# The four column tiles of each modulation product in reversed order, three of them pinned behind the one before

## The chip, the core and the metric

The kernel runs on one core of a Trainium2 chip. The metric is the device time of one execution in microseconds; the time before is the median of 3 runs, 1778.3 us (1777.71 to 1779.84). All data are float32.

## The reference, cut to what matters

One step of a two-layer diffusion backbone on 512 latent tokens and 128 context tokens, width 1024. Each layer derives six modulation vectors (shift, scale and gate, for attention and for the feed-forward part) from two conditioning vectors, `c` for latent and `c_ctx` for context tokens:

```
def modulation(cond, w_mod, b_mod):
    m = jax.nn.silu(cond) @ w_mod + b_mod        # (N, 1024) @ (1024, 6144)
    return jnp.split(m[:, None, :], 6, axis=-1)
...
h = rms_norm(x, norm_attn) * (1.0 + sc_a) + sh_a
proj = h @ w_in                                  # then two kinds of attention
x = x + g_a * (attention(proj) @ w_out)
h = rms_norm(x, norm_ffn) * (1.0 + sc_f) + sh_f
gate, up = jnp.split(h @ w_gate_up, 2, axis=-1)
x = x + g_f * ((jax.nn.silu(gate) * up) @ w_down)
```

The change touches only how `silu(cond) @ w_mod` is computed; the large products, `h @ w_in` and the like, run on the same engine around it.

## The kernel before

Activations are kept transposed, channels on the 128 partitions. Every large product is done three times with operands split into a high and a low part (`prod`, L476 to L478): ScalarE copies the high part of a weight (L83, tile `whi`), VectorE subtracts to get the low part (L84, `wlo`), and TensorE accumulates high by high, high by low and low by high. A weight tile comes by DMA from SyncE's queue (L449, `raw`, two buffers).

Order: `run` goes through start, projections, attention, output projection and feed-forward part of layer 0, then of layer 1. The modulation is laid beside the large products as generators: `step(side)` lets one advance by one `yield` after a block of products. Which instruction stands where in an engine's queue is then settled by the framework's scheduler, which plays the program through on a simulated timeline and prefers what was written earlier among what is ready. `tc.keep_in_program_order(ins)` adds one edge: `ins` may not be placed ahead of the instruction of its engine that was written last before it. It adds no semaphore and doesn't forbid others to come between.

Two parts compute modulation with column tiles, that is, products with only 32 output columns which use one quarter of TensorE's columns each. Tile j writes partitions 32j to 32j+31 of one accumulator (`mm`, two buffers).

- `mod` (L249), once, in the projections of layer 0, for 2048 of the 6144 columns. For each of 8 chunks k of 128 channels, four loads L263 of 256 KB bring 512 columns each into a `Q` buffer (six buffers in all), and four products L266 (weights `cT`, moving operand the loaded tile) accumulate into one bank. After k=7 VectorE copies the bank (L272), TensorE transposes it.
- `mod_sums` (L284), beside the output projection and the feed-forward part of layer 0, for the other eight groups of 1024 columns. VectorE multiplies each loaded chunk with the conditioning vector as a scalar per partition and adds up (L312 for k=0, L310 for the others, 128x512, four tiles `Q`, two for each conditioning vector), in eight steps of k. These sums are pinned with `keep_in_program_order`. Then `mod_store` (L321) sums over the partitions with four products L327 (weights `ones`, moving operand one of the four sums), copies the bank (L330, VectorE), transposes it (L333) and adds the bias (L339).

L619 and L643 are the end of the key heads on VectorE and the transposes of the keys on TensorE, L990 and L923 VectorE's readers of the large products in the feed-forward part.

Of the kernel before, what the change touches and what calls it, by code (L numbers as in the profile page):

```python
# [19 lines left out]
P = 128  # L20
D = 1024
KC = D // P
# [21 lines left out]
class Net:  # L44
# [153 lines left out]
    def start(self):  # L198
# [14 lines left out]
        acc = [self.S() for _ in range(3)]  # L213
        mod = self.start_mod(0)
        next(mod)
        for k in range(KC):
            next(mod)
            self.norm_scale(state, k)
            self.norm_chunk(state, k, 0, NT, rb)
            if k < KC - 1:  # L220
                mod = self.start_mod(k + 1)
                next(mod)
            if k % 2 == 0:
                wh = self.t([P, 2, 512], "whi", F32R, bufs=4)
                wl = self.t([P, 2, 512], "wlo", F32R, bufs=4)
                for b in range(2):
                    c = slice(256 * b, 256 * b + 256)
                    self.split(wh[:, :, c], wl[:, :, c], self.raw0[b][:, k:k + 2])
            for t in range(NTILE):
                o = acc[t // 2][:, 512 * (t % 2):512 * (t % 2) + 512]  # L230
                c, w = slice(t * P, (t + 1) * P), k % 2
                for i, (l_, r_) in enumerate(((hi, wh), (hi, wl), (lo, wh))):
                    nc.tensor.matmul(o, lhsT=l_[k][:, c], rhs=r_[:, w], start=k == 0 and i == 0,  # L233
                                     stop=k == KC - 1 and i == 2)
# [14 lines left out]
    def mod(self, l, g, place):  # L249

        nc = self.nc
        acc = self.mm()
        for k in range(KC):
            src = self.ins["w_mod"][l, k * P:(k + 1) * P, g * 2048:(g + 1) * 2048]
            if place == "Q":
                dst = [self.t([P, 512], "Q", bufs=6) for _ in range(4)]
            else:
                if k == 0:
                    self.ring = self.t([P, 2, 2048], "V")
                dst = [self.ring[:, k % 2]]  # L260
            n = 2048 // len(dst)
            for i, d in enumerate(dst):
                nc.sync.dma_start(d, src[:, i * n:(i + 1) * n])  # L263
            for j in range(4):
                c = j * 512
                nc.tensor.matmul(acc[32 * j:32 * j + 32, :], lhsT=self.cT[:, k, :],  # L266
                                 rhs=dst[c // n][:, c % n:c % n + 512],
                                 start=(k == 0), stop=(k == KC - 1), tile_position=(0, 32 * j))
            if k < KC - 1:
                yield  # L270
        m = self.t([P, 512], "P", bufs=3)
        nc.vector.tensor_copy(m, acc)  # L272
        pt = self.mm()
        for i in range(4):
            nc.tensor.transpose(pt[:, i * P:(i + 1) * P], m[:, i * P:(i + 1) * P], self.ident)
        for c in range(2):

            src = pt.rearrange("p (i j c) -> p j i c", i=4, j=4)[:, :, :, c]
            dst = self.modT[l][:, 16 * g:16 * g + 16, c].rearrange("p (j i) -> p j i", i=4)
            bias = self.vec[l][:, 16 * g:16 * g + 16].rearrange("p (j i) -> p j i", i=4)  # L280
            nc.vector.tensor_tensor(dst, src, bias, ALU.add)
        yield
# [38 lines left out]
    def mod_store(self, l, which, acc):  # L321
        nc = self.nc
        s = self.mm()
        for c in range(2):
            for i in range(2):
                j = 32 * (2 * c + i)
                nc.tensor.matmul(s[j:j + 32], lhsT=self.ones.broadcast_to([P, 32]), rhs=acc[c][i], start=True,  # L327
                                 stop=True, tile_position=(0, j))
        m = self.t([P, 512], "P", bufs=3)
        nc.vector.tensor_copy(m, s)  # L330
        pt = self.mm()
        for i in range(4):
            nc.tensor.transpose(pt[:, i * P:(i + 1) * P], m[:, i * P:(i + 1) * P], self.ident)  # L333
        for c in range(2):

            src = pt.rearrange("p (i c h r) -> p c h i r", i=4, c=2, h=2)[:, c, :, :, 0]
            dst = self.modT[l][:, KC * which:KC * which + KC, c].rearrange("p (h i) -> p h i", i=4)
            bias = self.vec[l][:, KC * which:KC * which + KC].rearrange("p (h i) -> p h i", i=4)
            nc.vector.tensor_tensor(dst, src, bias, ALU.add)  # L339
# [750 lines left out]
```

## Time and profile before

| | |
|---|---|
| median of 3 runs | 1778.3 us (1777.71 to 1779.84) |
| the profiled execution | 1776.35 us, its span 1774.6 us |
| TensorE busy | 1724.7 us (97%) |
| VectorE busy | 1014.1 us (57%) |
| ScalarE, GpSimd busy | 615.6 us, 277.6 us |
| granted TensorE clock, mean | 0.989 |

Times inside the profile are microseconds from the start of the span. A matmul's record lasts from its issue to the modelled end of its result, so records of one engine overlap, and the pitch from start to start tells what an instruction costs in a stream. In the timeline neighbours of one line are merged: "x2" with one duration is a run of two records.

### The profile page before, as it was taken

The numbers are of one execution on the slowest core, as the hardware profiler recorded it, in microseconds if no ns is written. First come the engines' busy times: TensorE is split into PE (matmuls) and PEld (weight loads), VectorE is DVE, ScalarE is ACT, GpSimd is POOL, SyncE is SP. The second block draws the span as 40 slices with busy tenths as digits, with TensorE's granted clock in tenths as the row PEclk, the third lists the DMA queues.
The fourth block names the chain that finished last, engine by engine and source line by source line (L and its number), as shares of the span: only waits on it lengthen the run. The fifth ranks groups of instructions, "written<-read, shape, count | busy, mean of one in ns | idle before, by whom it ended". The sixth has DMA issues, their size and how long they took to land.

```text
span 1774.6 us, 29153 instructions
## 1 busy us (share of the span) xinstructions
PE 1724.7 (97%) x12194; PEld 1609.7 (91%) x12194; DVE 1014.1 (57%) x1757; ACT 615.6 (35%) x1143; POOL 277.6 (16%) x266
## 2 busy tenths in 40 slices
PE   8889999999999999999999998999999999999999
PEld 6767978888999999899999997888999999999998
DVE  5765667877577877723247885778463232223222
ACT  4422376732422121212235434767252212221220
POOL 0332634400000000000002354453010000000000
PEclk9999999999999999999999999999999999999999
DMA  9343211153155554412222211112212222121212
GB/s 350 109 154 98 55 25 25 49 182 127 56 187 168 162 201 154 145 70 72 77 82 86 81 34 45 31 40 75 72 48 95 72 72 78 66 96 51 93 54 78
DMA packets 44259, 169.20 MB, mean 95 GB/s; under 512 B 5600, under 2 KB 8416, under 8 KB 32864
## 3 DMA queue, kind: packets, MB, share of 16 engines
q1 hardware_dynamic: 44128, 167.34, 28.5%
q8 instruction: 96, 1.57, 0.4%
q14 instruction: 35, 0.29, 0.1%
HBM read 152.90 MB, written 3.93 MB: 88 GB/s over the span
## 4 chain that ended last, share of the span: by engine, by line
PE 91%; DVE 3%; ACT 3%; DMA 1%; issue 1%; POOL 1%; SPq 0%; DVEq 0%; POOLq 0%; ACTq 0%
PE S L476 23%; PE S L477 23%; PE S L478 23%; PE S L687 3%; PE mm L792 3%; PE S L771 2%; PE S L688 2%; PE mm L327 2%; PE mm L788 2%; PE S L233 2%; PE mm L266 1%; PE mm L476 1%; PE mm L477 1%; PE mm L478 1%; DVE mx L707 1%
## 5 line engine op out<-in xcount | busy, mean ns | idle before, releaser
L83 ACT ACTIVATE whi<-raw 128x1024 fp32r<-128x1024 f32 (+2 forms) x192 | 196.2, 1025 | 811.2 <-PE S L477 734.8
L477 PE MATMUL S<-q,whi 128*128 128x256 f32 (+1 forms) x1408 | 436.3, 310 | 0.0
L478 PE MATMUL S<-k,wlo 128*128 128x256 f32 (+1 forms) x1408 | 434.6, 309 | 0.0
L476 PE MATMUL S<-k,whi 128*128 128x256 f32 (+1 forms) x1408 | 432.5, 310 | 1.5 <-ACT k L86 1.4
L84 DVE TENSOR_TENSOR wlo<-raw,whi 128x1024 fp32r<-128x1024 f32 (+2 forms) x192 | 229.9, 1200 | 183.1 <-ACT whi L83 175.9
L476 PEld LDWEIGHTS S<-k,whi 128*128 128x128 f32 x1408 | 265.5, 189 | 12.4 <-issue 10.1
L477 PEld LDWEIGHTS S<-q,whi 128*128 128x128 f32 x1408 | 266.7, 189 | 4.2 <-issue 4.2
L478 PEld LDWEIGHTS S<-k,wlo 128*128 128x128 f32 x1408 | 266.0, 189 | 2.5 <-issue 2.5
L478 PE MATMUL S<-hi,wlo 128*128 128x384 f32 (+1 forms) x768 | 237.9, 310 | 0.0
L477 PE MATMUL S<-lo,whi 128*128 128x384 f32 (+1 forms) x768 | 237.7, 310 | 0.0
L476 PE MATMUL S<-hi,whi 128*128 128x256 f32 (+1 forms) x768 | 237.7, 311 | 0.0
L923 DVE SCALAR_TENSOR_TENSOR x<-S,modT,x 128x128 f32<-128x128 f32 (+2 forms) x137 | 66.4, 524 | 208.6 <-PE S L478 208.6
L310 DVE SCALAR_TENSOR_TENSOR Q<-V,cT,Q 128x512 f32<-128x512 f32 x224 | 152.3, 743 | 0.0
L476 PE MATMUL S<-whi,hi 128*128 128x256 f32 x512 | 147.6, 288 | 1.9 <-ACT Q L241 1.9
L476 PEld LDWEIGHTS S<-hi,whi 128*128 128x128 f32 x768 | 144.0, 188 | 5.9 <-issue 5.0
L478 PEld LDWEIGHTS S<-hi,wlo 128*128 128x128 f32 x768 | 144.5, 188 | 3.4 <-issue 3.4
L478 PE MATMUL S<-whi,lo 128*128 128x256 f32 x512 | 145.8, 286 | 0.0
L477 PE MATMUL S<-wlo,hi 128*128 128x256 f32 x512 | 145.8, 285 | 0.0
L707 DVE TENSOR_REDUCE mx<-S 128x1 f32<-128x768 f32 x128 | 119.1, 950 | 46.3 <-PE S L688 46.0
L477 PEld LDWEIGHTS S<-lo,whi 128*128 128x128 f32 x768 | 144.4, 188 | 0.8 <-issue 0.8
L990 DVE TENSOR_TENSOR P<-S,P 128x640 f32<-128x640 f32 x44 | 36.2, 823 | 148.1 <-PE S L478 148.1
L476 PEld LDWEIGHTS S<-whi,hi 128*128 128x128 f32 x512 | 97.8, 191 | 8.2 <-issue 3.4
(206 smaller groups left out, 2820.7 us busy)
## 6 DMA issues: line engine op xcount, KB each, us to landing
raw<-in_w_gate_up SPq DMA_DIRECT2D x44, 1024.0 KB, 4.8
V<-in_w_mod SPq DMA_DIRECT2D x64, 512.0 KB, 3.9
raw<-in_w_in SPq DMA_DIRECT2D x16, 1024.0 KB, 4.8
raw<-in_w_down SPq DMA_DIRECT2D x16, 1024.0 KB, 5.0
Q<-in_w_mod SPq DMA_DIRECT2D x32, 256.0 KB, 3.1
raw<-in_w_out SPq DMA_DIRECT2D x8, 1024.0 KB, 5.1
raw<-in_w_down SPq DMA_DIRECT2D x8, 768.0 KB, 4.3
raw<-raw SPq DMA_DIRECT2D x40, 128.0 KB, 2.2
```

The source lines that it names most:

```text
L83: nc.scalar.activation(hi, src, AF.Copy)
L84: nc.vector.tensor_tensor(lo, src, hi.bitcast(F32), ALU.subtract)
L233: nc.tensor.matmul(o, lhsT=l_[k][:, c], rhs=r_[:, w], start=k == 0 and i == 0, stop=k == KC - 1 and i == 2)
L310: ins = nc.vector.scalar_tensor_tensor(a, v, self.cT[:, k, c:c + 1], a, ALU.mult, ALU.add)
L476: self.nc.tensor.matmul(out, lhsT=lh, rhs=rh, start=(i == 0), stop=False)
L477: self.nc.tensor.matmul(out, lhsT=lh, rhs=rl, start=False, stop=False)
L478: self.nc.tensor.matmul(out, lhsT=ll, rhs=rh, start=False, stop=(i == n - 1))
L687: nc.tensor.matmul(out, lhsT=Q[j][:, cols], rhs=keys[:, k0:k0 + n], start=True, stop=False)
L707: nc.vector.tensor_reduce(mx, s[:, 0:n], AX.X, ALU.max, negate=True)
L792: nc.tensor.matmul(o[64 * j:64 * j + 64], lhsT=self.V[:, v, 512 + 64 * j:576 + 64 * j], rhs=pts[j][:, i * P:(i + 1) * P], start=first, sto ...
L923: self.nc.vector.scalar_tensor_tensor(x[:, s:e], src[:, s - a:e - a], self.m(l, which, mb, c), x[:, s:e], ALU.mult, ALU.add)
L990: nc.vector.tensor_tensor(sg, out[1], sg, ALU.mult)
```

## The change

In `mod` and in `mod_store` the four column tiles are written in the order 3, 2, 1, 0 in place of 0 to 3, and tiles 2, 1 and 0 are each pinned behind the product written before, which is the next higher tile. Tile 3 is not pinned. Operands, shapes, loads and sums stay the same.

```diff
             for i, d in enumerate(dst):
                 nc.sync.dma_start(d, src[:, i * n:(i + 1) * n])
-            for j in range(4):
+            for j in reversed(range(4)):
                 c = j * 512
-                nc.tensor.matmul(acc[32 * j:32 * j + 32, :], lhsT=self.cT[:, k, :],
-                                 rhs=dst[c // n][:, c % n:c % n + 512],
-                                 start=(k == 0), stop=(k == KC - 1), tile_position=(0, 32 * j))
+                ins = nc.tensor.matmul(acc[32 * j:32 * j + 32, :], lhsT=self.cT[:, k, :],
+                                       rhs=dst[c // n][:, c % n:c % n + 512],
+                                       start=(k == 0), stop=(k == KC - 1), tile_position=(0, 32 * j))
+
+                if j < 3:
+                    self.tc.keep_in_program_order(ins)
...
     def mod_store(self, l, which, acc):
         nc = self.nc
         s = self.mm()
-        for c in range(2):
-            for i in range(2):
-                j = 32 * (2 * c + i)
-                nc.tensor.matmul(s[j:j + 32], lhsT=self.ones.broadcast_to([P, 32]), rhs=acc[c][i], start=True,
-                                 stop=True, tile_position=(0, j))
+
+        for j in reversed(range(4)):
+            ins = nc.tensor.matmul(s[32 * j:32 * j + 32], lhsT=self.ones.broadcast_to([P, 32]), rhs=acc[j // 2][j % 2],
+                                   start=True, stop=True, tile_position=(0, 32 * j))
+            if j < 3:
+                self.tc.keep_in_program_order(ins)
```

## Rows read from the trace of the kernel before

**Rows 1.** The page: TensorE's busy time and share; shares of the chain that ended last.

```profile
PE 1724.7 (97%) x12194; PEld 1609.7 (91%) x12194; DVE 1014.1 (57%) x1757; ACT 615.6 (35%) x1143; POOL 277.6 (16%) x266
...
PE 91%; DVE 3%; ACT 3%; DMA 1%; issue 1%; POOL 1%; SPq 0%; DVEq 0%; POOLq 0%; ACTq 0%
```

**Rows 2.** L266 and L327 by themselves: duration in ns (least/median/most), first and last start.

```profile
L266 PE MATMUL mm<-Q,cT x64: 592/605/617, 80.9 to 160.5; 128*32 128x512 f32 x64
...
L327 PE MATMUL mm<-Q,ones x64: 592/604/617, 418.6 to 758.0; 128*32 128x512 f32 x64
```

**Rows 3.** TensorE's timeline, a lone tile of L266: start, duration, line, tiles.

```profile
118.51 0.28 PE L477 MATMUL S<-wlo,hi 128*128 128x256 f32 x1
118.63 0.28 PE L478 MATMUL S<-whi,lo 128*128 128x256 f32 x1
118.84 1.04 PE L266 MATMUL mm<-Q,cT 128*32 128x512 f32 x2
...
120.04 0.28 PE L477 MATMUL S<-wlo,hi 128*128 128x256 f32 x1
```

**Rows 4.** TensorE's timeline, a lone tile of L327.

```profile
517.92 0.34 PE L477 MATMUL S<-q,whi 128*128 128x384 f32 x1
518.10 0.34 PE L478 MATMUL S<-k,wlo 128*128 128x384 f32 x1
518.37 1.05 PE L327 MATMUL mm<-Q,ones 128*32 128x512 f32 x2
...
519.63 0.34 PE L477 MATMUL S<-q,whi 128*128 128x384 f32 x1
```

**Rows 5.** TensorE's timeline, four tiles of L266 together.

```profile
152.93 0.28 PE L478 MATMUL S<-whi,lo 128*128 128x256 f32 x1
153.14 1.06 PE L266 MATMUL mm<-Q,cT 128*32 128x512 f32 x8
...
154.36 0.28 PE L477 MATMUL S<-wlo,hi 128*128 128x256 f32 x1
```

**Rows 6.** TensorE's timeline, the three runs of L266 for k=0.

```profile
80.87 1.05 PE L266 MATMUL mm<-Q,cT 128*32 128x512 f32 x2
...
85.18 1.05 PE L266 MATMUL mm<-Q,cT 128*32 128x512 f32 x2
...
103.03 1.05 PE L266 MATMUL mm<-Q,cT 128*32 128x512 f32 x4
```

**Rows 7.** TensorE's timeline, the last run of L327.

```profile
757.57 1.04 PE L327 MATMUL mm<-Q,ones 128*32 128x512 f32 x2
```

**Rows 8.** VectorE's timeline: the end of the sums before two stores.

```profile
507.07 2.73 DVE L310 SCALAR_TENSOR_TENSOR Q<-V,cT,Q 128x512 f32<-128x512 f32 x4
509.73 0.81 DVE L990 TENSOR_TENSOR P<-S,P 128x640 f32<-128x640 f32 x1
510.46 0.74 DVE L310 SCALAR_TENSOR_TENSOR Q<-V,cT,Q 128x512 f32<-128x512 f32 x1
...
746.94 4.06 DVE L310 SCALAR_TENSOR_TENSOR Q<-V,cT,Q 128x512 f32<-128x512 f32 x6
```

**Rows 9.** Busy time from 480 to 760 us; waits from 400 to 770 and 480 to 760.

```profile
480.00:760.00 280.00, 280.00 (x1762) 250.57 (x1761) 217.40 (x326) 55.13 (x62) 0.00 (x0) 1.00 0.51 166
...
DVE P L330 <- PE mm L327: 32.7, 8, 7.8
...
DVE P L990 <- PE S L478: 13.6, 9, 4.9
```

**Rows 10.** All of TensorE's waits from 80 to 165 us: total, times, longest.

```profile
PE S L643 <- DVE Q L619: 7.6, 2, 4.1
PE mm L476 <- ACT P L554: 0.2, 1, 0.2
```

**Rows 11.** SyncE's waits for L266, 70 to 170 us; loads L263, 97 to 165 us.

```profile
SPq L263 <- PE mm L266: 44.2, 21, 6.1
...
Q<-in_w_mod SPq DMA_DIRECT2D x27, 256.0 KB, 3.1
```

## The prediction

> **What bounds the kernel now.** I read the page's engine shares first: TensorE is busy for 97% of the span, and the chain that ended last runs through it for 91% [rows 1]. So a TensorE microsecond saved counts wherever nothing else is about to end a wait. Next come the two lines that change. L266 and L327 are 64 matmul records each, that is 32 products each, as every float32 product with 32 output columns leaves two records of 0.6 us [rows 2]. Records overlap, so their duration is no price. The price is read from TensorE's order of time.
>
> There the reader sees the same shape again and again: score or weight products at a steady pitch, one column tile ("x2"), more products, the next column tile. Around a lone tile of L266 the products start at 118.63 and, two products on, at 120.04: 1.41 us in place of two pitches of 0.12, so the tile costs 1.17 us [rows 3]. Around a lone tile of L327 among products of 384 columns the two starts are 518.10 and 519.63: 1.53 us against two pitches of 0.18, again 1.17 us [rows 4]. Where all four tiles of a step stand together ("x8", 1.06 us) the same pair of starts is 152.93 and 154.36: 1.43 less 0.24 is 1.19 us [rows 5]. Two tiles together show 1.05 us, as one alone does [rows 6]. **So the cost is per run of column tiles, not per tile**: 1.17 us for each run, plus about 0.02 where it holds four.
>
> **How many runs go.** Counted on the timeline, the eight k steps of L266, from 80.87 to the last records at 160 us, stand in 23 runs: three for k=0, two for k=1, four each for k=2 to 5, one each for k=6 and 7 [rows 2, 5, 6]. The eight stores of L327, from 418.6 to 758.0, stand in four runs each, 32 in all; the last begins at 757.57 [rows 2, 7]. With one run per step and per store 16 stay: 15 and 24 go.
>
> **The change part by part.** *The reversed order* lets the tile whose operand comes last go first, so that the other three are ready when it is issued. *The pins* forbid the three to stand before it. They don't say that nothing comes between: on VectorE, whose sums are pinned in this way already, L990 stands between two sums [rows 8]. I take it that the four stay together from other rows: every lone tile stands in the middle of a chain of products that were ready [rows 3, 4], so a ready column tile is put ahead of products, and four that were ready together did stay together without any pin [rows 5].
>
> *What is removed.* 24 runs of L327 by 1.17 are 28.1 us. All stores but the first lie between 480 and 760 us, where TensorE is busy for 280.00 of 280 us, so each counts in full [rows 9]; the first stands in a chain of products too. Of the 15 runs of L266 two give nothing: those at 80.87 and 85.18 come before TensorE's two waits for VectorE's L619, 7.6 us together, which grow by what is saved ahead of them [rows 6, 10]. 13 by 1.17 are 15.2 us. Sum: 43.3 us, less 0.02 for each of the 14 groups that grow to four, 0.3: **43.0 us**. No instruction is added and no DMA is moved.
>
> By its column-tile rows the price of a group is 1.19 us. The Trainium skill ("TensorE: Matmul & The Clock Gate", Part 3, "What overlaps and what doesn't") says that a weight load overlaps matmuls in flight only where the row group differs. All four tiles here contract over all 128 rows, so by that sentence they take turns, the sum is nothing and the time stays at 1778; the x8 run of rows 5 speaks against it.
>
> *Waits added.* The first issued tile stands at the head of TensorE's queue, and all products behind it wait if its operand is late. For a store this operand is the last sum. At the 512 us store it ends at 510.46 + 0.74 = 511.20 and the fourth run starts at 518.37 [rows 4, 8]; at the last store the sums end at 746.94 + 4.06 = 751.00 and the fourth run starts at 757.57 [rows 7, 8]. The slot comes 3.5 us earlier (three runs gone), which leaves 6.57 - 3.5 = 3.1 us at the nearer of the two: I take nothing. With that margin gone and one sum of 0.74 late at every store it is 8 x 0.74 = 6 us.
>
> For L266 the operand is a 256 KB load, 3.1 us from issue to landing [rows 11]. TensorE never waited for one: from 80 to 165 us its list names L619 and one ScalarE result alone [rows 10]. But the four buffers now come free together, and the last two loads of the next step start only then; SyncE already waits 44.2 us for L266 in that stretch, in 21 waits of up to 6.1 us [rows 11]. Weight loads are queued behind these loads on SyncE; no product waited for one there [rows 10]. I take nothing, as the row of TensorE's waits is the nearest to it; the worst is one landing at each of seven later steps, 7 x 3.1 = 22 us.
>
> *VectorE.* It is busy for 217.4 of the 280 us from 480 to 760 [rows 9]. With 21 runs by 1.17 = 24.6 us less, that is 217.4 of 255.4, or 85%. Its waits stand where time goes: the eight copies L330 of a store wait 32.7 us for the column tiles, L990 13.6 us for products [rows 9]. These shrink first. The next part's third and fourth sums reuse the buffers of the store, and now wait for the whole group rather than for its first two tiles, up to three runs or 3.5 us longer. The copy's wait, 4.1 us on average, covers that. I take nothing; uncovered at every store it is 8 x 3.5 = 28 us, and then the gain of the stores is just given back.
>
> Against the profiled execution: 1776.35 - 43.0 = 1733.4. The median of the runs shown lies 1.95 us above it, so **1735 us**. Bounds: all 39 runs count (45.6 us, 1733), and an altered queue order may help a little too, 5 us further down. Above, the worst ends of 6, 22 and 28 us exclude each other in part, since VectorE waits are shorter where TensorE stands; a third of their sum is 19 us (1754).
>
> **Rivals.**
> *Partly given back* (0.18): groups split where another matmul is as urgent, or the late buffers and VectorE's 85% bind in places. For it: L990 between pinned sums [rows 8], the SyncE waits [rows 11]. Against: TensorE's short list of waits [rows 10]. Half the gain gives 1778.3 - 21.5 = 1757; the case spans 1745 to 1770.
>
> *The pins don't hold them together* (0.05): the next tile counts as ready only when a product has already taken the slot, so four runs stay, only shifted: 1778. For it: pinned sums are split too [rows 8]. Against: most of them stand together, six in one row [rows 8].
>
> *Column tiles of a store take turns* (0.02): L327 shows only single tiles, so their overlap is not seen, and at 1.17 us each the 24 runs give nothing. L266's 13 runs would still give 15.2 us: 1763; if those took turns as well, 1778. Against: same shape, same durations as L266 [rows 2], whose x8 run takes 1.06 us [rows 5]. The sentence of the Trainium skill quoted above would be this case in its second form.
>
> *Slower* (0.05): the in-order wait at a store's head. If the last sum came later against TensorE by one more step of eight sums (at the pitch of the x6 row, (4.06 - 0.74) / 5 = 0.66 us, 5.3 us) and by one more wait of the kind that L330 shows now (4.1 us), 9.4 us together, TensorE would stand for 9.4 - 3.1 = 6.3 us at each of eight stores: 50 us against 43, or 1785. It turns to a loss at 3.1 + 43 / 8 = 8.5 us of shift. Against: every copy L330 waits for TensorE today [rows 9], so VectorE is ahead at each store.
>
> **How the numbers follow.** The forecast, full grouping with the gain passed on (1728 to 1745), has 0.70; the rivals 0.18, 0.05, 0.02 and 0.05. About 0.2% (3.5 us) is what a measurement can tell here. Faster: 0.70 + 0.18 + 0.01 of the column-tile case = 0.89; same 0.06; slower 0.05. The range of 1728 to 1754 holds the forecast and about half of the partial case, so nearly 0.8.
>
> **What would show it.** Right: L266 and L327 in eight runs each, all x8, of 1.05 to 1.07 us; TensorE's records unchanged in number and duration; the products of 165 us some 15 us earlier and those of 760 us some 43; L330's waits well below 32.7 us; no wait of TensorE for L310, L312 or a w_mod load. Wrong: x2 runs left; a wait of TensorE at L266 or L327 of a microsecond or more; or waits for a split L84 in the feed-forward part, which would mean that VectorE has become the bound.

## The result, and the profile after

The changed kernel takes **1745.17 us** (median of 4 runs, 1743.89 to 1746.24). The kernel before, run beside it, takes 1778.01 us (1774.44 to 1779.84). The ratio is 0.9819, with a 95% interval of 0.9803 to 0.9834: 32.8 us faster. The forecast was 1735 us, a gain of 43, with a range of 1728 to 1754. Sign and range hold; ten microseconds of the forecast gain did not come. The question of this study is where they went.

The profiled execution took 1744.55 us. The lines of the code have moved: L327 is now L329, L330 is L334, L310 is L313, L476 to L478 are L480 to L482, L619 is L623, L643 is L647, L663 is L667, L687 is L691. L263, L266, L83 and L84 stand where they stood. The page, first the engines' busy time, then the chain of waits, answers to [rows 1]:

```profile
PE 1684.9 (97%) x12194; PEld 1608.8 (92%) x12194; DVE 1014.6 (58%) x1757; ACT 615.4 (35%) x1143; POOL 277.9 (16%) x266
...
PE 88%; DVE 5%; ACT 3%; DMA 2%; POOL 1%; issue 1%; SPq 0%; POOLq 0%; DVEq 0%; ACTq 0%
```

The same 12194 matmul records keep TensorE busy for 39.8 us less, so more than the whole gain left its busy time. But its share of the chain fell from 91% to 88%, and VectorE's rose from 3% to 5%: part of what was saved has become waiting. The two changed lines by themselves, against [rows 2]:

```profile
L266 PE MATMUL mm<-Q,cT x64: 592/605/617, 114.1 to 157.7; 128*32 128x512 f32 x64
```

```profile
L329 PE MATMUL mm<-Q,ones x64: 592/604/617, 418.6 to 728.5; 128*32 128x512 f32 x64
```

L329 ends 29.5 us earlier than L327 did. L266 **begins 33 us later** than before, at 114.1 in place of 80.9. All of TensorE's waits from 80 to 165 us answer to [rows 10]:

```profile
PE S L647 <- DVE Q L623: 12.2, 2, 9.3
PE mm L266 <- DMA Q<-in_w_mod: 1.5, 2, 1.2
```

So the wait for the heads is 4.6 us longer than before, and at two groups of L266 the products now stand for a load, 1.5 us together. All groups are complete, as TensorE's timeline shows at two modulation steps and at the store that answers to [rows 4]:

```profile
114.06 1.07 PE L266 MATMUL mm<-Q,cT 128*32 128x512 f32 x8
115.06 0.39 PE L480 MATMUL mm<-whi,hi 128*128 128x256 f32 x1
...
146.55 1.07 PE L266 MATMUL mm<-Q,cT 128*32 128x512 f32 x8 [1.16 <-DMA Q<-in_w_mod]
```

```profile
510.32 1.06 PE L329 MATMUL mm<-Q,ones 128*32 128x512 f32 x8
511.31 0.39 PE L480 MATMUL S<-k,whi 128*128 128x256 f32 x1
```

Each line stands in eight groups, all x8, of 1.06 to 1.07 us. The waits from 400 to 760 us answer to the list of L330 and L990 in [rows 9] (in total, times, longest):

```profile
DVE P L334 <- PE mm L329: 17.2, 4, 5.0
DVE P L994 <- PE S L482: 12.4, 8, 4.9
...
DVE Q L315 <- PE mm L329: 8.0, 3, 3.9
...
PE mm L391 <- DVE rstd L101: 4.0, 1, 4.0
...
PE S L480 <- ACT P L991: 0.7, 1, 0.7
```

The store's copy waits 17.2 us in four waits, in place of 32.7 in eight: ahead of the other four copies VectorE no longer stood idle. The two rows of PE are all that TensorE waits for in this stretch, so no product waits for a sum of VectorE (L313, L315).

**Where on the time axis the gain arises.** Matmuls of large products were counted in order of time, and equal places compared (equal counts, as the blocks' order is not the same everywhere). Three places matter: the 601st, late in the projections, with the last of L266 done in both kernels; the 841st, the first of the output projection; and the 3385th, the first of layer 1's projections, where all the modulation is over. TensorE's timelines show the rows, the kernel before first:

```profile
178.99 0.37 PE L476 MATMUL S<-whi,hi 128*128 128x256 f32 x1
...
367.68 0.36 PE L476 MATMUL S<-hi,whi 128*128 128x256 f32 x1
...
790.64 0.28 PE L476 MATMUL S<-hi,whi 128*128 128x256 f32 x1
```

```profile
169.11 0.37 PE L480 MATMUL mm<-whi,hi 128*128 128x256 f32 x1
...
364.90 0.49 PE L480 MATMUL S<-hi,whi 128*128 128x256 f32 x1
...
760.52 0.28 PE L480 MATMUL S<-hi,whi 128*128 128x256 f32 x1
```

At the first place the changed kernel is 9.9 us ahead (169.11 against 178.99), at the second 2.8, at the third 30.1. So the stores gave 30.1 - 2.8 = **27.3 us**. The reversed steps of L266 gave 9.9 us, of which **7.1 were lost again** between there and the output projection.

### The profile page after: what moved, and what is told of

Its sections match the earlier page's. It is cut to its first block, busy times and chain, and to the rows that moved or that the text cites. A ratio compares the mean times of both kernels' runs of the same rounds, so it can differ in the third digit from the quotient of the medians.

```text
span 1742.8 us, 29150 instructions
## 1 busy us (share of the span) xinstructions
PE 1684.9 (97%) x12194; PEld 1608.8 (92%) x12194; DVE 1014.6 (58%) x1757; ACT 615.4 (35%) x1143; POOL 277.9 (16%) x266
## 4 chain that ended last, share of the span: by engine, by line
PE 88%; DVE 5%; ACT 3%; DMA 2%; POOL 1%; issue 1%; SPq 0%; POOLq 0%; DVEq 0%; ACTq 0%
PE S L481 23%; PE S L480 23%; PE S L482 23%; PE S L691 3%; PE mm L796 3%; PE S L775 3%; PE S L692 2%; PE mm L792 2%; PE S L233 2%; ACT whi L743 1%; DVE mx L711 1%; DMA V<-in_w_mod 1%; DMA raw<-in_w_out 1%; DMA Q<-in_w_mod 1%; PE mm L480 1%
## 5 line engine op out<-in xcount | busy, mean ns | idle before, releaser
L83 ACT ACTIVATE whi<-raw 128x1024 fp32r<-128x1024 f32 (+2 forms) x192 | 196.3, 1026 | 780.9 <-PE S L481 707.7
L482 PE MATMUL S<-k,wlo 128*128 128x256 f32 (+1 forms) x1408 | 433.6, 308 | 0.0
L480 PE MATMUL S<-k,whi 128*128 128x256 f32 (+1 forms) x1408 | 430.3, 309 | 2.2 <-ACT k L86 1.4
L84 DVE TENSOR_TENSOR wlo<-raw,whi 128x1024 fp32r<-128x1024 f32 (+2 forms) x192 | 229.1, 1196 | 175.8 <-ACT whi L83 167.8
L480 PEld LDWEIGHTS S<-k,whi 128*128 128x128 f32 x1408 | 264.9, 189 | 3.9 <-ACT k L86 1.6
L482 PEld LDWEIGHTS S<-k,wlo 128*128 128x128 f32 x1408 | 265.3, 189 | 0.0
L481 PE MATMUL S<-lo,whi 128*128 128x256 f32 (+1 forms) x768 | 237.8, 310 | 0.0
L482 PE MATMUL S<-hi,wlo 128*128 128x256 f32 (+1 forms) x768 | 237.5, 310 | 0.0
L480 PE MATMUL S<-hi,whi 128*128 128x256 f32 (+1 forms) x768 | 237.2, 311 | 0.0
L313 DVE SCALAR_TENSOR_TENSOR Q<-V,cT,Q 128x512 f32<-128x512 f32 x224 | 152.5, 744 | 0.0
L480 PE MATMUL S<-whi,hi 128*128 128x256 f32 x512 | 148.2, 290 | 3.8 <-ACT Q L241 1.9
L482 PE MATMUL S<-whi,lo 128*128 128x256 f32 x512 | 146.7, 288 | 0.0
L480 PEld LDWEIGHTS S<-hi,whi 128*128 128x128 f32 x768 | 144.2, 188 | 0.8 <-issue 0.8
L482 PEld LDWEIGHTS S<-hi,wlo 128*128 128x128 f32 x768 | 144.5, 188 | 0.0
L480 PEld LDWEIGHTS S<-whi,hi 128*128 128x128 f32 x512 | 98.8, 193 | 6.3 <-ACT Q L241 2.2
```

The source lines that it names most:

```text
L83: nc.scalar.activation(hi, src, AF.Copy)
L84: nc.vector.tensor_tensor(lo, src, hi.bitcast(F32), ALU.subtract)
L313: ins = nc.vector.scalar_tensor_tensor(a, v, self.cT[:, k, c:c + 1], a, ALU.mult, ALU.add)
L480: self.nc.tensor.matmul(out, lhsT=lh, rhs=rh, start=(i == 0), stop=False)
L481: self.nc.tensor.matmul(out, lhsT=lh, rhs=rl, start=False, stop=False)
L482: self.nc.tensor.matmul(out, lhsT=ll, rhs=rh, start=False, stop=(i == n - 1))
```

## The experiments

Two theories were put against each other; the expectations call them A and B. **A**: the loss comes from the order that the reversed modulation steps bring. A reversed step needs all four loads at once, the modulation therefore starts late, and work that stood well moves with it. **B**: the loss lies in the head work (norm, rotation and transposes of queries and keys on VectorE and GpSimd), which is not ready earlier in any order, so that a lead of TensorE is always stopped at attention. One table holds all results; "ahead" is the lead over the kernel before at the three places just named.

| kernel | median, us | before beside it | ratio, 95% interval | ahead at 601st | ahead at output projection | ahead at layer 1 |
|---|---|---|---|---|---|---|
| changed | 1745.17 | 1778.01 | 0.9819 (0.9803 to 0.9834) | 9.9 | 2.8 | 30.1 |
| store_only | 1749.01 | 1778.26 | 0.9837 (0.9822 to 0.9852) | -0.7 | 0.6 | 28.0 |
| mod_only | 1776.78 | 1778.26 | 0.9991 (0.9981 to 1.0000) | 10.7 | 3.7 | 2.5 |
| k0_old | 1742.61 | 1778.26 | 0.9802 (0.9785 to 0.9818) | 14.8 | 10.1 | 37.2 |
| k01_old | 1737.19 | 1778.26 | 0.9770 (0.9755 to 0.9785) | 11.8 | 8.9 | 36.0 |
| rev_nopin | 1742.0 (one run) | 1777.37 | | 10.3 | 5.0 | 32.5 |
| open_early | 1746.62 | 1777.37 | 0.9828 (0.9812 to 0.9844) | 12.5 | 4.7 | 31.1 |
| pt_s | 1746.54 | 1777.37 | 0.9826 (0.9808 to 0.9843) | 2.2 | 3.7 | 30.8 |
| k01_pt_s | 1737.52 | 1777.37 | 0.9778 (0.9764 to 0.9793) | 10.7 | 11.6 | 39.8 |
| pin_norev | 1779.39 (one run) | 1777.73 | | -2.4 | -2.8 | -2.7 |
| store_pairs | 1757.99 | 1777.73 | 0.9890 (0.9875 to 0.9904) | 8.1 | 3.3 | 20.8 |
| before_pt_s | 1777.71 | 1777.73 | 1.0002 (0.9993 to 1.0012) | -0.6 | -0.5 | -0.6 |
| k0_pt_s | 1743.4 | 1777.73 | 0.9812 (0.9796 to 0.9828) | 6.5 | 8.0 | 35.4 |

The places come from one execution each. Equal order can differ by some 2 us already before the first modulation step (pin_norev, whose products run in the order of the kernel before, is 2.1 us late there), so single microseconds in the last three columns are not read. Nor do the leads stand still behind layer 1's first product, though the modulation is over there: at the last product of all k0_old is 34.6 us ahead in place of 37.2, pt_s 27.7 in place of 30.8, k01_old 37.4 in place of 36.0.

### The two halves of the change

store_only reverses the stores alone; mod_only reverses the steps of `mod` alone. (In each the other loop is as before the change.)

> The stores alone have the reversed order and the pins; the eight steps of mod are as before. All theories: the stores give their whole term, 24 runs of column tiles by 1.17 us, so 1778 - 28 = 1750 us, within 2. If the two places help or hinder each other, it is off by more than that.

> mod alone has the reversed order and the pins; the stores are as before. The prediction's step (13 runs by 1.17 us counted in full) would give 1778 - 15 = 1763 us. Theory A (a reversed step needs four free load buffers at once, so mod starts later, its accumulator opens later, and what was won is lost before and at the start of attention) and theory B (the start of attention is bound by VectorE's and GpSimd's work on the heads, whatever TensorE saves before it) both say 1778 less 3 to 5, so 1773 to 1775 us.

The stores alone give 28.0 us at layer 1 and 29.3 by the medians: the term of 28.1 holds, and nothing of it is given back. The modulation steps alone are 10.7 us ahead at the 601st product, 3.7 at the output projection and 1.5 by the medians, a smaller gain than any expectation had. The shortfall belongs to L266 entirely.

**The price by itself.** store_pairs lets two tiles of a store stand together and not four, so that each store has two runs:

```diff
-        for j in reversed(range(4)):
+        for j in (1, 0, 3, 2):
...
-            if j < 3:
-                self.tc.keep_in_program_order(ins)
```

> The changed kernel with the four tiles of a store in the order 1, 0, 3, 2, which leaves two runs of two at each store instead of one run of four. By the price of a run, 8 runs more by 1.17 us: 9.4 us above the changed kernel, 1754 to 1756 us. If a tile had its own price besides the run's, or if part of the gain came from the order of the sums, it is off by 2 us or more.

The timeline shows the two runs of the second store as x4, both of 1.05 us:

```profile
508.68 1.05 PE L329 MATMUL mm<-Q,ones 128*32 128x512 f32 x4
...
512.11 1.05 PE L329 MATMUL mm<-Q,ones 128*32 128x512 f32 x4
```

From the output projection to layer 1 it gains 20.8 - 3.3 = 17.5 us, the changed kernel 27.3. Eight more runs cost 9.8 us, 1.23 each: the cost is per run, whether two tiles stand in it or four. The whole time is 2 to 4 us above what was expected. Most of that does not lie in the stores: from layer 1's first product to the last of all its lead falls from 20.8 to 18.9 us, and the changed kernel's grows from 30.1 to 31.8. Why was not tried.

### Which half of the edit acts

rev_nopin keeps the reversed order and drops both pins; pin_norev keeps the old order and pins tiles 1 to 3.

```diff
-                if j < 3:
-                    self.tc.keep_in_program_order(ins)
```

```diff
-            for j in reversed(range(4)):
+            for j in range(4):
...
-                if j < 3:
+                if j > 0:
```

> The changed kernel without its six pinned tiles' edges: the order 3, 2, 1, 0 alone. If the pins hold the tiles together, they come apart and the time goes back towards 1778 us. If the products of one accumulator keep their written order anyway, the reversal does it all: eight runs of four at each place and 1745 us, within 2.

> The kernel before with the pins (tiles 1, 2 and 3 behind the one before) but in the old order 0, 1, 2, 3. If it is the reversal that does it, the runs stay 23 and 32 and the time is that of before, 1774 to 1780 us.

Without pins every engine has the same instructions in the same order as in the changed kernel, and with pins alone the order is that of the kernel before. **The pins do nothing; the reversal is the change.** The four products write one accumulator, and here they keep their written order anyway (that the common accumulator is the reason is not shown). rev_nopin's one run, 1742.0 us, lies a microsecond below what was expected and 1.9 below the shortest of the changed kernel's four: executions of one order lie that far apart, so 2 or 3 us between two kernels are not read as a gain further down. In the old order tile 0, whose operand comes first, went first, and the other three followed as their operands came; reversed, the tile that is ready last opens the group.

### What the late start takes along

Two rows of the kernel before and two of the changed one, TensorE's timeline from 80 to 96 us (the bracket names the idle time ahead of a row and what ended it):

```profile
82.14 0.39 PE L476 MATMUL mm<-whi,hi 128*128 128x256 f32 x1 [0.22 <-ACT P L554]
...
90.29 0.74 PE L643 MATMUL S<-ident,Q 128*128 128x128 f32 x5 [4.06 <-DVE Q L619]
```

```profile
90.49 1.30 PE L647 MATMUL S<-ident,Q 128*128 128x128 f32 x5 [9.35 <-DVE Q L623]
...
95.04 1.30 PE L647 MATMUL S<-ident,Q 128*128 128x128 f32 x5 [2.82 <-DVE Q L623]
```

Before, a block of 24 products into an `mm` bank started at 82.14, in time in which TensorE would otherwise have waited for the key heads (L619). In the changed kernel that block runs at 115.06, right behind the first group of L266 (the second row of the fence further up): its `mm` bank comes behind the one of the modulation's accumulator, and that one is taken only at 114.06. So the wait for the heads is 9.35 us long, with 12.2 in the stretch in place of 7.6, and the 24 products at a pitch of 0.12, 2.9 us, stand later in the open. The granted clock falls earlier; stretches of 5 us, before and after (busy time and count of PE, PEld, DVE, ACT and POOL, then the granted clock, DMA share and GB/s):

```profile
85.00:90.00 5.00, 1.23 (x5) 0.18 (x3) 4.96 (x7) 0.45 (x2) 5.00 (x4) 1.00 0.05 15
```

```profile
85.00:90.00 5.00, 0.00 (x0) 0.00 (x0) 4.97 (x8) 0.00 (x0) 5.00 (x4) 0.53 0.05 15
90.00:95.00 5.00, 1.73 (x7) 1.36 (x7) 4.72 (x14) 1.82 (x2) 2.31 (x3) 0.50 0.78 277
```

With TensorE idle over the whole of the first stretch the granted clock is down at 0.53 and then 0.50, the lower of its two levels (1.2 GHz); before, the fall came one stretch later (0.64 from 90 to 95 us). What this costs was not measured by itself, and store_only, with the old order here, has 0.92 and 0.50 in these two stretches.

The first group waits that long for its buffers. SyncE's waits from 70 to 170 us answer to [rows 11]:

```profile
SPq L263 <- PE S L647: 16.5, 5, 10.3
SPq L263 <- DMA Q<-in_w_mod: 15.3, 7, 4.1
SPq L263 <- PE mm L266: 10.8, 7, 2.5
```

The key heads hold `Q` buffers until L647 has transposed them. Before, tiles of k=0 passed one after another through what was free; a reversed step needs four buffers at once.

Four experiments take this apart. k0_old leaves k=0 in the old order, k01_old k=0 and k=1:

```diff
-            for j in reversed(range(4)):
+            for j in range(4) if k == 0 else reversed(range(4)):
...
-                if j < 3:
+                if k and j < 3:
```

```diff
+            for j in range(4) if k < 2 else reversed(range(4)):
...
+                if k > 1 and j < 3:
```

> The changed kernel, but step k=0 of mod in the old order and without pins; k=1 to 7 and the stores stay changed. Theory A: k=0 again goes tile by tile through the one free buffer from about 81 us on, the accumulator opens there, the 24 products of the fourth block's last token tile return into TensorE's wait of 9 us for L623 (2.85 us saved), mod ends 6 to 10 us earlier, and attention starts 3 to 10 us earlier: 1735 to 1742 us. Theory B: the 2.85 us are lost again at the start of attention: 1744 to 1746 us.

> The changed kernel, but steps k=0 and k=1 of mod in the old order and without pins. Theory A: as with k=0 alone, one run of column tiles more (1.2 us) against a start that frees buffers sooner: 1735 to 1743 us. Theory B: 1744 to 1747 us.

open_early keeps the change whole, and adds one product that opens the accumulator when it is taken (its result is overwritten by k=0):

```diff
         acc = self.mm()
+        nc.tensor.matmul(acc[0:32, 0:P], lhsT=self.cT[:, 0, :], rhs=self.ident,
+                         start=True, stop=True, tile_position=(0, 0))
```

> The changed kernel with one more column-tile product (32x128, ready from the start, its result overwritten) ahead of mod's first load, so that the accumulator's bank is taken early and the 24 products of the fourth block's last token tile can go back into the wait for L623. Loads and groups of mod stay late. Theory A (what counts is when mod ends, as the sixth block's last token tile waits in written order for mod's bank and its transposes): mod still ends near 157 us and the 2.85 us won at 82 us are lost again: 1743.5 to 1746 us. If the lost cover alone is the cause: 1740 to 1742 us.

k0_old's L266 runs from 80.9 to 152.8, and it is 14.8 us ahead at the 601st product, with a time of 1742.61. **k01_old takes 1737.19 us, 8.0 less than the changed kernel**: with two steps in the old order, which stand in three and two runs, it is faster than with all eight steps grouped. That lies within what A expected (k0_old half a microsecond above it). In the profiled executions, 5.6 us apart, all of it is there at layer 1, where k01_old is 5.9 us ahead of the changed kernel. But k0_old, 1.2 us further ahead at that place than k01_old, takes 5.4 us longer (2.8 in the profiled executions): it falls back in layer 1, where its order on TensorE differs from that of the other two. Two of its waits from 1200 to 1450 us are not in k01_old's list:

```profile
PE S L480 <- ACT P L991: 0.7, 1, 0.7
PE S L481 <- DVE q L87: 0.6, 1, 0.6
```

So what sets k0_old and k01_old apart does not lie in the modulation steps. In open_early the 24 products are back inside the wait:

```profile
83.76 0.38 PE L482 MATMUL mm<-whi,hi 128*128 128x256 f32 x1 [1.19 <-ACT P L560]
```

Its lead at the 601st product is 12.5 us, 2.6 more than the changed kernel's; part of that can be the loads, for which no product of L266 waits there. So the order in which the banks are taken is what moves that block. But its lead at the output projection is 4.7 and its time 1746.62, 0.6 above A's range: the lost cover is real, and it does not set the time. What it gives back is lost at attention.

### The loss at the start of attention

Stretches from 190 to 200 us, first of the kernel before, then of the changed one:

```profile
190.00:200.00 10.00, 10.00 (x86) 9.79 (x85) 4.89 (x6) 2.15 (x4) 7.91 (x8) 1.00 0.07 15
```

```profile
190.00:200.00 10.00, 7.73 (x51) 7.10 (x51) 7.17 (x9) 3.93 (x8) 8.83 (x10) 0.90 0.38 94
```

TensorE was busy throughout; now it waits at times, with a chain through the heads' work on GpSimd and VectorE (L620, L622, L623) ahead of it, and at its end this wait:

```profile
196.37 0.59 ACT PT L678
```

```profile
PE S L480 <- ACT PT L678: 1.9, 1, 1.9
```

The granted clock of 0.90 is not the reason. rev_nopin, which has the same order on every engine, was granted 1.00 in each stretch of 10 us from 190 to 240, and loses nearly as much:

```profile
190.00:200.00 10.00, 7.71 (x59) 7.08 (x58) 7.17 (x9) 3.91 (x8) 8.83 (x10) 1.00 0.41 102
```

A place inside attention parts the loss, the first product of L818 (L822 in the changed kernel). TensorE's timelines of the kernel before, the changed one and rev_nopin:

```profile
249.04 1.09 PE L818 MATMUL S<-wlo,V 128*64 128x128 f32 x16 [0.71 <-ACT P L709]
```

```profile
244.72 1.09 PE L822 MATMUL S<-wlo,V 128*64 128x128 f32 x16 [0.71 <-ACT P L713]
```

```profile
243.86 1.09 PE L818 MATMUL S<-wlo,V 128*64 128x128 f32 x16 [0.71 <-ACT P L709]
```

The leads there are 4.3 and 5.2 us, so from the 601st product on the changed kernel has lost 5.6 and rev_nopin 5.1. From there to the output projection the one loses the other 1.5 of its 7.1, and rev_nopin 0.2. In that part the granted clocks differ: 0.84 against 1.00 from 355 to 365 us.

By B the heads' work is all there is to it. pt_s tests that. After k=7 the four transposes of `mod`'s result take an `mm` bank as well, in the middle of the projections; here they go into half of an `S` buffer, of which there are three:

```diff
-        pt = self.mm()
+        pt = self.S()[:, 0:512]
```

The same line is changed in k01_pt_s (on k01_old), k0_pt_s (on k0_old) and before_pt_s (on the kernel before).

> The changed kernel, but mod's four transposes write a bank of the score pool instead of a bank of the two mm buffers, so that no block's last token tile waits behind the end of mod. Theory A: the heads of the sixth block are finished earlier, attention starts 3 to 6 us earlier: 1739 to 1742 us. Theory B (head work on VectorE and GpSimd bounds the start of attention in any order): 1744 to 1746 us.

> Steps k=0 and k=1 of mod in the old order, and the transposes in a bank of the score pool. Theory A: both gains add in part: 1730 to 1736 us. Theory B: as steps 0 and 1 in the old order alone, 1736 to 1739 us.

> The kernel before with mod's transposes in a bank of the score pool, nothing else. Theory A: TensorE is the bound there before, the heads of the sixth block are not late for it, so no gain: 1775 to 1780 us.

> The changed kernel with step k=0 of mod in the old order and mod's transposes in a bank of the score pool. Theory A: the first keeps the 24 products under the wait for L623 and lets mod start early (14.8 us ahead after the first 600 products), the second keeps that lead over the start of attention: 1733 to 1737 us. If the lead is lost again to waits for loads, as with the transposes moved alone, 1737 to 1742 us.

In the kernel before the line is worth nothing (1.0002). Between the 601st product and the output projection the changed kernel loses 7.1 us, k0_old 4.7, k01_old 2.9; with this line pt_s, k0_pt_s and k01_pt_s lose nothing and gain 1.5, 1.5 and 0.9. In k01_pt_s, the same stretch:

```profile
190.00:200.00 10.00, 10.00 (x81) 9.75 (x80) 4.28 (x7) 2.61 (x6) 3.53 (x3) 1.00 0.29 66
```

GpSimd's timeline shows what moved: the second row of L613 after 140 us (the gain multiplied onto a pair of query heads), in the kernel before (L609), in the changed kernel, in k01_old and in k01_pt_s:

```profile
174.75 3.05 POOL L609 TENSOR_TENSOR q<-q,small 128x640 f32<-128x640 f32 x2 [17.90 <-DVE q L607]
```

```profile
174.25 3.05 POOL L613 TENSOR_TENSOR q<-q,small 128x640 f32<-128x640 f32 x2 [24.32 <-DVE q L611]
```

```profile
166.93 4.05 POOL L613 TENSOR_TENSOR q<-q,small 128x640 f32<-128x640 f32 x2 [19.54 <-DVE q L611]
```

```profile
158.88 3.06 POOL L613 TENSOR_TENSOR q<-q,small 128x640 f32<-128x640 f32 x2 [11.61 <-DVE q L611]
```

In the changed kernel GpSimd waits 24.32 us ahead of it for VectorE's part of the heads (L611); the row comes hardly earlier than in the kernel before, with TensorE 9.9 us ahead. In k01_pt_s it starts 15.4 us earlier. **B falls**: the same head work is ready in time in another order, and a lead of 10.7 us passes through the start of attention whole, where mod_only, with the same 10.7, loses some 7. By time, k01_old took 6.8 us less than the least that B allowed.

But that moving the transposes pays, as A had it, is borne out by none of the times. A's ranges for pt_s and k0_pt_s were missed by far, with 1746.54 and 1743.4, and k01_pt_s, with 1737.52, lies above A's range and in B's. In the first two the lead is gone before attention, 2.2 us at the 601st product in pt_s. TensorE's waits from 65 to 395 us in pt_s, and its timeline there:

```profile
PE mm L266 <- DMA Q<-in_w_mod: 3.9, 2, 3.4
```

```profile
156.23 1.94 PE L266 MATMUL mm<-Q,cT 128*32 128x512 f32 x8 [3.42 <-DMA Q<-in_w_mod]
```

```profile
155.00:160.00 5.00, 2.88 (x13) 1.15 (x14) 1.61 (x3) 0.00 (x0) 0.00 (x0) 0.50 0.09 36
160.00:165.00 5.00, 5.00 (x25) 5.00 (x25) 3.87 (x16) 0.00 (x0) 1.10 (x1) 0.50 0.01 3
```

The last group stands 3.42 us for its loads, its x8 takes 1.94 us in place of 1.06, and for two stretches the granted clock is 0.50. All products behind the group's head wait with it. k0_pt_s shows the same wait (3.40 us, at 152.83). In k01_pt_s the last group, at 150.84, finds its loads there. By their medians k01_pt_s (1737.52) and k01_old (1737.19) can't be told apart, although k01_pt_s is 2.8 us ahead at the output projection and 3.3 at the last product. The profiled executions differ by as much: 1738.93 us, the longest of k01_old's four, and 1735.67, the shortest of k01_pt_s's. So the trace shows that a lead can pass the start of attention whole, and not that the moved transposes make the kernel faster.

## Why the prediction was right, and where it was not

**Right: the price and the grouping.** A run of column tiles costs what the pairs of starts said: 1.17 us forecast, 1.23 measured by store_pairs for runs of two, and 1.14 by the 24 runs that went from the stores (27.3 us). Each of the 16 steps and stores became one x8 run. By the sentence of the Trainium skill ("TensorE: Matmul & The Clock Gate", Part 3, "What overlaps and what doesn't") that a weight load overlaps matmuls in flight only where the row group differs, they would take turns, since all four contract over the same rows. The measurement says otherwise: eight groups of L329 at 1.06 us, and 27.3 us saved by them.

**Right: the stores.** "24 runs of L327 by 1.17 are 28.1 us": 27.3 in the changed kernel, 28.0 at layer 1 with the stores alone. The zeros taken for a late last sum and for VectorE hold: no product waited for a sum, the copy's waits fell to 17.2 us, and the later reuse of the sums' buffers (L315 after L329) grew to 8.0 us on VectorE without reaching TensorE. In the kernel before the row reads:

```profile
DVE Q L312 <- PE mm L327: 2.7, 4, 1.4
```

**Wrong: "13 by 1.17 are 15.2 us."** It measured 9.9 us at the 601st product and 2.8 at the output projection; alone, the reversed steps are worth 1.5 us by the medians. Three steps of the working failed in it.

- "Of the 15 runs of L266 two give nothing" looked at the wait for L619 as a place that hides column tiles. It hid 24 large products too, whose bank depended on the tile removed from there. They cost about 2.9 us in the open, by their pitch.
- "the last two loads of the next step start only then", and yet "I take nothing": the rows listed no wait for a load because most tiles had gone one by one, as their loads came. Now TensorE waits for loads at two groups of L266, 1.5 us. The longer of them, 1.16 us at 146.55, is the sign that the prediction named for being wrong ("a wait of TensorE at L266 or L327 of a microsecond or more"). The bound of 22 us was far too wide, zero too narrow. Together these come to 15.2 - 2.9 - 1.5 = 10.8, against 9.9 measured; the last 0.9 is not assigned.
- The forecast ended its account at 165 us and passed the gain on. Nothing was asked about what stands ready at the start of attention. There 5.6 us were lost, and 1.5 more at the end of attention, in the execution that was profiled. k01_old and k01_pt_s, whose heads come earlier, lose 2.9 and nothing over the whole stretch: the loss depends on the order of the head work.

**Wrong without a price: "The pins forbid the three to stand before it."** They forbid nothing that was not fixed already.

Of the rivals, "partly given back" is the nearest: its mechanism of late buffers is one of the three causes, though its split groups and its VectorE bound are not. The measured 1745.17 lies on the border, just above the 1728 to 1745 of the forecast's own case (0.70) and just inside the 1745 to 1770 of this one (0.18). The stated range held it because it reached up to 1754 for worst ends of 6, 22 and 28 us, none of which came in that size; for the larger part of the loss the prediction had no term, so that it held is in part luck. What would have shown it was named: "the products of 165 us some 15 us earlier and those of 760 us some 43". The product that started at 165.00 was 11.5 us earlier (the changed kernel still had its last step of L266 to come there), the one at 759.96 was 30.2.

**Open.** What the lower clock costs at 85 to 95 us, why moving the transposes gains no time on k01_old, and why the leads move by up to 3 us in layer 1, are not settled.

## What to carry to other kernels

Price small column-tiled products by the run, not by the tile, and group them by writing the tile that is ready last first; no pin was needed here, where they share an accumulator. Before grouping, look at what the trickle of single tiles did: here the first two steps filled a wait, took a bank early and passed through one spare buffer, and leaving these two as they were makes 1737 us out of 1745. Follow a gain to the next place where another engine must deliver, since a lead that arrives there early may only wait.

## What was not expected of the hardware

The granted clock differs between executions of equal work. rev_nopin has the changed kernel's order on every engine; from 220 to 230 us TensorE was busy for 7.02 us there, and for 7.82 in the changed kernel. First the changed kernel, then rev_nopin:

```profile
220.00:230.00 10.00, 7.82 (x45) 6.43 (x44) 5.81 (x14) 8.39 (x29) 1.78 (x2) 0.83 0.01 2
```

```profile
220.00:230.00 10.00, 7.02 (x50) 5.80 (x49) 6.28 (x15) 8.17 (x29) 2.55 (x4) 1.00 0.01 2
```

The one ran at a mean of 0.83 and the other at 1.00, and from 355 to 365 us it is 0.84 against 1.00. In stretches where TensorE waits now and then, its clock, and with it some 2 us of the time, is a matter of the execution. A lead that is read from one trace of such a stretch needs a second one beside it.
